# A hybrid GLA and MLA decoder block in float32: one weight sum moved into accumulating transfers, one product order changed, one set of PSUM banks and one gate changed

## Chip, cores and metric

The kernel runs on one core of one Trainium2 chip. The metric is the device time of one execution in microseconds. An execution's time is a little longer than the span of its profile, from the first to the last instruction of the program.

## What is computed

One layer of an autoregressive decoder, with 512 tokens, a width of 1024, in float32 throughout. After a layer norm, two branches run on the same rows: gated linear attention (GLA, 4 heads) and multi-head latent attention (MLA, 8 heads with a nope part of 128 and a rotary part of 64). Each is projected back, the two are merged by sigmoid gates, and one output projection follows; then comes a squared-ReLU MLP. Cut to what matters:

```python
h = layer_norm(x, ln_in_g, ln_in_b)
q_g, k_g, v_g, r_g, a_lr, q_lat, kv_lat, gate_logits = jnp.split(h @ w_in, offsets, axis=-1)
o_gla = gla_chunked(...)                                  # 4 heads, chunks of 64
y_gla = (rms_norm(o_gla) * silu(r_g)) @ w_o_gla
q = (rms_norm(q_lat, q_a_norm_g) @ w_q_b).reshape(bsz, seq, MLA_HEADS, MLA_QK)
q_nope, q_rope = q[..., :128], apply_rope(q[..., 128:], cos, sin)
kv = (rms_norm(kv_lat) @ w_kv_b).reshape(...)             # nope keys and values of 8 heads
y_mla = merge_heads(mla_causal_attention(...)) @ w_o_mla
g_gla, g_mla = jnp.split(jax.nn.sigmoid(gate_logits + b_gate), 2, axis=-1)
h = layer_norm(ALPHA * h + (g_gla * y_gla + g_mla * y_mla) @ w_out)
h = layer_norm(ALPHA * h + jnp.square(jax.nn.relu(h @ w_ff1)) @ w_ff2)
```

## The kernel before, in words

**Split products.** Every float32 operand of a large product is split into a high part, rounded to the matmul's format, and a low part, the rest; a product is three matmuls (high by high, high by low, low by high). `split` and `pump` do this for activations and weights: ScalarE copies the high part, VectorE subtracts it. A row named `whi<-wraw` or `whi<-wq` in the profile is the first half of a weight split, `wlo<-...` the second. There are two `whi` and two `wlo` buffers and three raw ones, so the split of an element of the weight stream can begin when TensorE has finished the element two before it.

**The stream.** All weights pass through one list, `stream`, in the order in which `plan`, `plan_unit`, `plan_qr` and `plan_pair` append to it; the products must be called in the same order. `fetch` issues plain loads on the SP queue ahead of use, and `pump` splits one or two elements ahead. An element may carry `gates`: instructions of ScalarE or VectorE behind which its split is queued. An element may have a `post`, called once its split is issued.

**Seven products in place of eight.** The large square projections, among them GLA's output (`yg`, weights `w_o_gla`), are computed with a Winograd-like scheme: a 2 by 2 block product from seven products, with weight blocks 11, 22, 21 and the sums t1, t2, t3, t4. The sums are formed in the raw tiles (`wq`): t1 and t3 by loading one block and adding another to it with an accumulating transfer (issued by GpSimd, line 1308), t2 by a VectorE addition behind the split of 22 (`u_sum`). For `yg`, t4 is t2 plus block 21; before the change VectorE adds it behind the split of block 21. For the second gate unit (`g1`) t4 is made by `u_acc`, an accumulating transfer of block 21 from HBM onto the tile of t2 (line 412).

**MLA.** For each pair of heads, `mla_pair` makes nope queries, nope keys and values. `mla_qr(g)` makes the rotary queries of four heads: two accumulators are turned by cosine and sine tables on VectorE (rows `rt<-mm,tab`), split, and sent to their places by GpSimd transfers (`QS<-q`). The heads (`mla_head`) are generators that are stepped between products: scores (L1121 to L1132), softmax on VectorE and ScalarE, transposes of the probabilities (L1154, tile `Ps` or `P02`, evicted as `PT`), and outputs (L1175 to L1177).

**PSUM.** There are two pools of four banks: `mm`, for the accumulators of the projections (`MM()`), and `px` (`PX()`), for transposes, scores, attention outputs and some accumulators. The nope keys of the first pair stand in `px`, those of the other three in `mm`.

**Start.** The first layer norm's rows are normalised on ScalarE and VectorE, transposed on TensorE, scaled, and split into `h` by `ln_transpose`, one block of 128 features at a time for 256 tokens. `ln_in1` does this for the second half of the tokens, between the products for the latents.

**What sets the order.** Python's order of calls gives each instruction its priority. When the program is built, the framework orders each engine's instructions by that priority and by its own simulated timeline, gives out buffers and banks, and adds the semaphores. On the chip every engine works through its list in that fixed order. The kernel ties single instructions down with `issue_after`. The order around GLA's last products is, in the stream and in the calls:

```python
    t0, mv = mla_pair(0)
    mv()
    y_gla("21")
    mla_qr(1)
    y_gla("t4")
    t1, mv = mla_pair(1)
```

Of the kernel before, what the change touches and what calls it, by code (L numbers as in the profile page):

```python
# [52 lines left out]
def tile_hybrid_block(ctx: ExitStack, tc: tile.TileContext, I, out, dbg=None):  # L53
# [12 lines left out]
    def nm(s):  # L66
        uid[0] += 1
        return f"{s}_{uid[0]}"
# [18 lines left out]
    def MM(n="mm"):  # L87
        return pm.tile([P, T], F32, tag="mm", name=nm(n))

    def PX(shape=(P, T), dt=F32, n="px"):  # L90
        return px.tile(list(shape), dt, tag="px", name=nm(n))

    def f(ap):
        return ap.bitcast(F32)
# [46 lines left out]
    xt = []  # L141
# [14 lines left out]
    g_in = ca[:, P:P + NK]  # L156
    b_in = ca[:, P + NK:P + 2 * NK]
# [11 lines left out]
    stream = []  # L169
    st = {"dma": 0, "spl": 0, "gates": ()}  # L170
# [75 lines left out]
    def weights(pl, k):  # L246
        i, j = pl["at"][k]
        pump(i)
        hi, lo = stream[i]["w"]
        return hi[:, j, :], lo[:, j, :]  # L250
# [4 lines left out]
    def spawn(g):  # L255
        active.append(g)
        return g
# [22 lines left out]
    def gemm_fm(pl, xs, n, evac, width=None, toks=slice(0, T), accs=None, guard=None, held=False):  # L280
        na = n // P
        accs = accs or [MM() for _ in range(na)]
        for k in range(pl["nk"]):
            hi, lo = weights(pl, k)
            xh, xl = part(xs[k], 0, toks), part(xs[k], 1, toks)
            first, last = k == 0, k == pl["nk"] - 1
            for a in range(na):
                c = slice(a * P, (a + 1) * P)
                o = accs[a][:, toks]
                with ExitStack() as gates:  # L290
                    if last and held:
                        gates.enter_context(tc.issue_after(st["tp"].ins))
                    mm(o, hi[:, c], xh, start=first, stop=False)  # L293
                mm(o, hi[:, c], xl, start=False, stop=False)  # L294
                mm(o, lo[:, c], xh, start=False, stop=last)  # L295
            if not last:
                tick(width)
        if guard:
            guard()
        if evac is not None:  # L300
            for a in range(na):
                evac(a, accs[a])
                if a == na // 2 - 1:
                    pump(pl["idx"][-1] + 1)
        tick(width)
        return accs
# [45 lines left out]
    PL = {}  # L352
# [16 lines left out]
    for op, _ in RW:  # L369
        for hf in range(2):  # L370
            PL["r"].append(len(stream))
            e = {"nk": 2, "n": T, "res": False, "ahead": 2, "home": "wwwwrwrwrwwwrw"[2 * RW.index((op, _)) + hf]}
# [7 lines left out]
    def plan_qr(g):  # L380
        PL["qr", g] = plan("w_q_b", NOPE, 4 * ROPE, heads=(HQ, 4 * g, 4), parts=2)
# [21 lines left out]
    def u_sum(key, a, to, g, x, new=None):  # L403
        src = WQ[key, (a, g)]
        t = WQ[key, (to, g)] = src if new is None else new
        with tc.issue_after(st["lo"].ins):
            vtt(t, src, x, op=ALU.add)


    def u_acc(key, a, to, g, op):  # L410
        t = WQ[key, (to, g)] = WQ[key, (a, g)]
        nc.gpsimd.dma_start(t, u_src(key, int(op[0]) - 1, int(op[1]) - 1, g), accum_op=ALU.add)

    def plan_unit(*seq):
        for key, op in seq:
            for g in range(UNITS[key][2]):
                PL[key, op, g] = len(stream)
                e = {"nk": 4, "n": 256, "res": False}
                if key in ("g1","yg"):
                    e["cut"] = 2  # L420
                if (key, op, g) == ("yg", "t3", 1):
                    e["home"] = "b"
                if op[0] != "t" and (op, key) not in HELD:
                    e["dmas"] = [(slice(0, 4), u_src(key, int(op[0]) - 1, int(op[1]) - 1, g), None)]
                else:
                    e["src"] = lambda q=(key, (op, g)): WQ[q]
                    if key == "g0" and op in ("t1", "t2"):
                        e["ahead"], e["home"] = 2, "wr"[g]
                if op == ("t1" if key == "g0" else "22"):
                    e["post"] = lambda raw, q=(key, "t1", "t2", g): u_sum(*q, WQ[q[0], ("22", q[3])] if q[0] == "g0" else raw)  # L430
                    if key == "f1":
                        e["post2"] = lambda raw, q=(key, "12", "t3", g): u_sum(*q, raw)
                elif op == "21" and key == "yg":
                    e["post"] = lambda raw, g=g: u_sum("yg", "t2", "t4", g, raw)
                elif op == "t2" and key == "g1":
                    e["post"] = lambda raw, g=g: u_acc("g1", "t2", "t4", g, "21")
                elif op == "t2" and key != "yg":
                    e["post2" if key == "f1" else "post"] = lambda raw, q=(key, "t2", "t4", g): u_sum(*q, WQ[q[0], ("21", q[3])])
                stream.append(e)

# [10 lines left out]

    plan_pair(0)
    plan_unit(("yg", "21"))
    plan_qr(1)
    plan_unit(("yg", "t4"))
    plan_pair(1)
    plan_pair(2)
    plan_pair(3)
# [63 lines left out]
    def ln_transpose(rows, g, b, outs, hf, alt=False, n="h0"):  # L522
        tk = slice(hf * 256, (hf + 1) * 256)
        for k in range(NK):
            if len(outs) <= k:
                outs.append(A([P, 2, T], F32R, n) if n == "h0" else (B([P, T], F32R, n), B([P, T], F32R, n)))
            p = MM() if alt and k in (4, 5) else PX()
            for i in range(2):
                tp = nc.tensor.transpose(p[:, i * P:(i + 1) * P], rows[2 * hf + i][:, k * P:(k + 1) * P],
                                         identJ if hf and n == "h0" else ident)  # L530
            if k == 1:
                st["tp"] = tp
            tmp = B([P, 256], F32, "lnt")
            hi, lo = part(outs[k], 0, tk), part(outs[k], 1, tk)
            ha = act(hi, p[:, :256], AF.Identity, scale=g[:, k:k + 1], bias=b[:, k:k + 1])
            if (alt or n == "h1") and k % 2:
                act(tmp, p[:, :256], AF.Identity, scale=g[:, k:k + 1], bias=b[:, k:k + 1])
            else:
                vts(tmp, p[:, :256], g[:, k:k + 1], b[:, k:k + 1], op0=ALU.mult, op1=ALU.add)
            hd = vtt(lo, tmp, f(hi), op=ALU.subtract)  # L540
            if n == "h1":
                st["ln"] = (ha, hd)
            elif hf and k == 5:
                st["h0"] = (ha, hd)
            yield hd

    mvin = consts.tile([P, NT, 2], F32, name="mvin")
    hT = []
# [125 lines left out]
    qlT, ckT, qld, ckd, GL, KKs = [], [], [], [], [], []  # L674
# [413 lines left out]
    def mla_pair(pr):  # L1088
        vt = [None] * NT
        qn = [None] * 2  # L1090
        kn = [None] * 2

        def ev_v(a, j, ps):
            t = B([P, 2, 256], F32R, "mv")
            split(ps[:, :256], t[:, 0, :], t[:, 1, :])
            vt[a] = t

        def ev_n(dst, sc):
            def e(a, ps):
                dst[a] = A([P, 2, T], F32R, "qn")  # L1100
                split(ps, dst[a][:, 0, :], dst[a][:, 1, :], scale=sc)
            return e
        gemm_fm(PL["qn", pr], qlT, 256, ev_n(qn, scale))
        gemm_fm(PL["kn", pr], ckT, 256, ev_n(kn, None), accs=None if pr else [PX(), PX()])
        return ([spawn(mla_head(2 * pr + a, a, qn[a], kn[a], vt)) for a in range(2)],
                lambda guard=None: gemm_tm([PL["mv", pr]], ckT, 256, ev_v, guard=guard))

# [76 lines left out]
    def ln_in1():  # L1184
        for i in range(4):
            yield

        def splits():
            stream[5]["gates"] = (st["var"],)
            pump(4)  # L1190
            chain.update(dve=st["lo"])

        for tt in (2, 3):
            chain.update(dve=st["lo"] if tt == 2 else st["nmr"])
            ln_rows(xt[tt], xt[tt], mvin[:, tt, :], on_act=((0, 1), (0,))[tt - 2], between=splits if tt == 2 else None)
            chain.clear()
            if tt == 3:
                stream[7]["gates"] = (st["var"],)
            yield
            if tt == 2:  # L1200
                yield
        stream[PL["q"]["idx"][0]]["gates"] = (st["norm"],)
        yield from ln_transpose(xt, g_in, b_in, hT, 1, alt=False)

    hsd = []

# [261 lines left out]
    hT = hops = None  # L1468
# [32 lines left out]
    y_gla = unit("yg", yops, ev_y, after_y)  # L1501
# [2 lines left out]
    t0, mv = mla_pair(0)  # L1504
    mv()
    y_gla("21")
    mla_qr(1)
    y_gla("t4")
    ogT = yops = y_gla = None
    t1, mv = mla_pair(1)  # L1510
    mv(lambda: finish(*t0))
    t2, mv = mla_pair(2)
# [56 lines left out]
    accs = gemm_fm(PL["f1", 0, 0], h1T, T, None, toks=slice(0, 256), held=True)  # L1569
# [289 lines left out]
```

## Time and profile before

| what | us |
| --- | --- |
| median of 3 runs (lowest, highest) | 864.10 (864.09, 864.13) |
| the profiled execution's own time | 864.03 |
| its span | 862.2 |
| TensorE matmuls busy | 852.3 (99%) |
| TensorE weight loads busy | 752.8 (87%) |
| VectorE busy | 658.1 (76%) |
| ScalarE busy | 494.0 (57%) |
| GpSimd busy | 136.0 (16%) |
| granted TensorE clock, mean | 0.998 |

Times in the profile count from the first instruction. Matmuls are pipelined and their ends are modelled, so their rows overlap: the step from one start to the next tells more than a row's length. PE is TensorE, PEld its weight loads, DVE VectorE, ACT ScalarE, POOL GpSimd, SP the queue of plain loads. A row of the timeline has start, length, engine, line, operation, output and inputs, shape, count, and in brackets the idle time before it and what ended that. Most VectorE and ScalarE instructions go through one helper and bear its line, L111, so they are told apart by their tiles. The later parts of the program, from the output projection (about 480 us) on, are not touched.

### The profile page before, as it was taken

The numbers are of one execution on the slowest core, as the hardware profiler recorded it, in microseconds if no ns is written. First come the engines' busy times: TensorE is split into PE (matmuls) and PEld (weight loads), VectorE is DVE, ScalarE is ACT, GpSimd is POOL, SyncE is SP. The second block draws the span as 40 slices with busy tenths as digits, with TensorE's granted clock in tenths as the row PEclk, the third lists the DMA queues.
The fourth block names the chain that finished last, engine by engine and source line by source line (L and its number), as shares of the span: only waits on it lengthen the run. The fifth ranks groups of instructions, "written<-read, shape, count | busy, mean of one in ns | idle before, by whom it ended". The sixth has DMA issues, their size and how long they took to land.

```text
span 862.2 us, 13265 instructions
## 1 busy us (share of the span) xinstructions
PE 852.3 (99%) x4887; PEld 752.8 (87%) x4887; DVE 658.1 (76%) x1169; ACT 494.0 (57%) x891; POOL 136.0 (16%) x179
## 2 busy tenths in 40 slices
PE   8999999999999999999999999999999999999996
PEld 7988888889999999988888889888888888889985
DVE  7767889977578968997856879985567546898865
ACT  7456977655576754565645325475466446766810
POOL 1530001010211103030000021005301520141000
PEclk9999999999999999999999999999999999999999
DMA  9995946696649917143146355009922990599312
GB/s 316 233 214 156 341 156 161 211 263 219 148 134 249 211 43 183 44 105 98 42 177 217 115 165 189 1 1 266 256 63 57 299 222 9 107 249 229 112 61 74
DMA packets 101232, 137.94 MB, mean 160 GB/s; under 512 B 13202, under 2 KB 66117, under 8 KB 101169
## 3 DMA queue, kind: packets, MB, share of 16 engines
q1 hardware_dynamic: 76512, 91.35, 33.8%
q0 software_dynamic: 22784, 41.10, 22.9%
q10 hardware_dynamic: 1872, 4.66, 1.5%
q8 instruction: 38, 0.62, 0.3%
q14 instruction: 26, 0.20, 0.1%
HBM read 113.49 MB, written 8.91 MB: 142 GB/s over the span
## 4 chain that ended last, share of the span: by engine, by line
PE 97%; ACT 1%; DVE 1%; DMA 0%; issue 0%; POOLq 0%; POOL 0%; DVEq 0%
PE mm L293 10%; PE mm L295 10%; PE mm L294 10%; PE mm L1335 6%; PE mm L1333 6%; PE mm L1334 6%; PE mm L333 5%; PE mm L331 5%; PE mm L332 5%; PE px L1668 3%; PE px L1667 3%; PE px L1669 3%; PE mm L1668 2%; PE mm L1667 2%; PE mm L1669 2%; PE mm L887 1%
## 5 line engine op out<-in xcount | busy, mean ns | idle before, releaser
L111 DVE TENSOR_TENSOR wlo<-wraw,whi 128x1024 fp32r<-128x1024 f32 (+2 forms) x108 | 96.8, 911 | 63.3 <-ACT whi L111 63.2
L111 ACT ACTIVATE whi<-wraw 128x1024 fp32r<-128x1024 f32 (+2 forms) x108 | 85.1, 806 | 78.7 <-PE mm L294 19.3
L294 PE MATMUL mm<-h,whi 128*128 128x512 f32 x224 | 87.2, 389 | 0.0
L293 PE MATMUL mm<-h,whi 128*128 128x512 f32 x224 | 87.1, 390 | 0.0
L295 PE MATMUL mm<-h,wlo 128*128 128x512 f32 x224 | 83.2, 390 | 0.0
L111 DVE TENSOR_TENSOR wlo<-wq,whi 128x1024 fp32r<-128x1024 f32 (+1 forms) x66 | 63.6, 979 | 25.7 <-ACT whi L111 25.5
L111 ACT ACTIVATE whi<-wq 128x1024 fp32r<-128x1024 f32 (+1 forms) x66 | 55.3, 860 | 31.2 <-PE mm L1334 15.3
L1686 POOL DMA_DIRECT2D res<-ev x42 | 38.5, 1045 | 177.5 <-ACT ev L111 147.5
L1333 PE MATMUL mm<-sh,whi 128*128 128x256 f32 x176 | 49.9, 284 | 0.0
L1334 PE MATMUL mm<-sh,whi 128*128 128x256 f32 x176 | 49.7, 283 | 0.0
L293 PEld LDWEIGHTS mm<-h,whi 128*128 128x128 f32 x224 | 42.1, 188 | 8.7
L295 PEld LDWEIGHTS mm<-h,wlo 128*128 128x128 f32 x224 | 42.0, 188 | 8.7
L294 PEld LDWEIGHTS mm<-h,whi 128*128 128x128 f32 x224 | 42.0, 188 | 8.7
L1335 PE MATMUL mm<-sh,wlo 128*128 128x256 f32 x176 | 49.5, 283 | 0.0
L111 ACT ACTIVATE xh<-wraw 128x1024 fp32r<-128x1024 f32 (+1 forms) x24 | 24.2, 1016 | 25.4 <-PE mm L333 15.1
L111 ACT ACTIVATE relu<-mm 128x512 f32<-128x512 f32 x26 | 15.2, 594 | 37.5 <-PE mm L295 37.5
L111 DVE TENSOR_TENSOR xl<-wraw,xh 128x1024 fp32r<-128x1024 f32 (+1 forms) x24 | 27.9, 1170 | 11.2 <-ACT xh L111 11.1
L1334 PEld LDWEIGHTS mm<-sh,whi 128*128 128x128 f32 x176 | 33.8, 192 | 0.0
L1333 PEld LDWEIGHTS mm<-sh,whi 128*128 128x128 f32 x176 | 33.8, 192 | 0.0
L1335 PEld LDWEIGHTS mm<-sh,wlo 128*128 128x128 f32 x176 | 33.6, 192 | 0.0
L1335 PE MATMUL mm<-h,wlo 128*128 128x256 f32 x112 | 32.1, 287 | 0.0
L1333 PE MATMUL mm<-h,whi 128*128 128x256 f32 x112 | 31.8, 284 | 0.0
(495 smaller groups left out, 2785.6 us busy)
## 6 DMA issues: line engine op xcount, KB each, us to landing
wraw<-in_w_ff_dram SPq DMA_DIRECT2D x36, 512.0 KB, 5.4
wraw<-in_w_in_dram SPq DMA_DIRECT2D x30, 512.0 KB, 5.2
wq<-in_w_ff_dram POOLq DMA_DIRECT2D x26, 512.0 KB, 11.2
res<-ev POOLq DMA_DIRECT2D x42, 256.0 KB, 9.1
wq<-in_w_in_dram POOLq DMA_DIRECT2D x20, 512.0 KB, 9.5
wq<-in_w_in_dram SPq DMA_DIRECT2D x18, 512.0 KB, 8.0
hsd<-hs SPq DMA_DIRECT2D x16, 256.0 KB, 4.2
xr<-hsd SPq DMA_DIRECT2D x16, 256.0 KB, 3.8
```

The lines of the kernel that those rows point to most:

```text
L111: ins = op(*a, **k)
L293: mm(o, hi[:, c], xh, start=first, stop=False)
L294: mm(o, hi[:, c], xl, start=False, stop=False)
L295: mm(o, lo[:, c], xh, start=False, stop=last)
L331: mm(o, xh, hi[:, :n], start=opens, stop=False, skip_group_check=share)
L332: mm(o, xh, lo[:, :n], start=False, stop=False, skip_group_check=share)
L333: mm(o, xl, hi[:, :n], start=False, stop=last, skip_group_check=share)
L1333: mm(oa, hi[:, k, c], xh, start=opens and k == 0 and a == 0, stop=False, skip_group_check=True)
L1334: mm(oa, hi[:, k, c], xl, start=False, stop=False, skip_group_check=True)
L1335: mm(oa, lo[:, k, c], xh, start=False, stop=k == 3, skip_group_check=True)
L1667: mm(o, xh[:, c], hi[:, pp], start=opens, stop=False, skip_group_check=True)
L1668: mm(o, xh[:, c], lo[:, pp], start=False, stop=False, skip_group_check=True)
```

## The change

Four edits.

1. GLA's output: the sum t4 = t2 + block 21 is no longer added by VectorE behind the split of 21. `u_acc` sends two accumulating transfers from HBM (one for each column group, 512 KB each) on GpSimd's queue, behind the split of t2. Block 21 is still loaded plainly for its own product.
2. The product t4 comes directly behind the product 21, in the stream and in the calls, and the second rotary queries behind it.
3. The second pair's nope keys accumulate in two `px` banks in place of two `mm` banks, as the first pair's do.
4. In `ln_in1` the split of the first query weights is queued behind the fourth transposed block of the second token half (its high part on ScalarE, its low part on VectorE), and not behind the last normalisation on ScalarE.

```diff
-                elif op == "21" and key == "yg":
-                    e["post"] = lambda raw, g=g: u_sum("yg", "t2", "t4", g, raw)
-                elif op == "t2" and key == "g1":
-                    e["post"] = lambda raw, g=g: u_acc("g1", "t2", "t4", g, "21")
-                elif op == "t2" and key != "yg":
+                elif op == "t2" and key in ("g1", "yg"):
+                    e["post"] = lambda raw, key=key, g=g: u_acc(key, "t2", "t4", g, "21")
+                elif op == "t2":
...
     plan_unit(("yg", "21"))
+    plan_unit(("yg", "t4"))
     plan_qr(1)
-    plan_unit(("yg", "t4"))
...
             hd = vtt(lo, tmp, f(hi), op=ALU.subtract)
+            st["ha"] = ha
...
-        gemm_fm(PL["kn", pr], ckT, 256, ev_n(kn, None), accs=None if pr else [PX(), PX()])
+        gemm_fm(PL["kn", pr], ckT, 256, ev_n(kn, None), accs=None if pr > 1 else [PX(), PX()])
...
-        stream[PL["q"]["idx"][0]]["gates"] = (st["norm"],)
-        yield from ln_transpose(xt, g_in, b_in, hT, 1, alt=False)
+        for k, hd in enumerate(ln_transpose(xt, g_in, b_in, hT, 1, alt=False)):
+            if k == 3:
+                stream[PL["q"]["idx"][0]]["gates"] = (st["ha"], hd)
+            yield
...
     y_gla("21")
+    y_gla("t4")
     mla_qr(1)
-    y_gla("t4")
```

## The prediction

> **What bounds the kernel now.** I read the page first, then the list of waits for the two halves of TensorE, then busy time by stretch, and last the timeline at the few places where TensorE stood. The page says that TensorE carries the time.
>
> ```profile
> span 862.2 us, 13265 instructions
> ...
> PE 852.3 (99%) x4887; PEld 752.8 (87%) x4887; DVE 658.1 (76%) x1169; ACT 494.0 (57%) x891; POOL 136.0 (16%) x179
> ...
> PE 97%; ACT 1%; DVE 1%; DMA 0%; issue 0%; POOLq 0%; POOL 0%; DVEq 0%
> ```
>
> The profiled execution took 864.03 us, its span 862.2 plus 1.83 around it; the runs have a median of 864.10 (864.09 to 864.13), 0.07 above. I make the sum against 864.03. The change removes no matmul, so it can only win time in which TensorE stands. The waits of the weight loads, which show a stall earlier than the modelled ends of matmuls do, name nearly all of it after the start (one more, at 28 us, has its own rows below):
>
> ```profile
> PEld mm L293 <- ACT PT L111: 0.8, 1, 0.8
> ...
> PEld mm L295 <- DVE wlo L111: 0.4, 1, 0.4
> ...
> PEld px L1175 <- DVE PT L111: 0.4, 1, 0.4
> PEld px L1176 <- DVE PT L111: 0.4, 1, 0.4
> ```
>
> ```profile
> 360.00:370.00 10.00, 9.64 (x58) 8.25 (x56) 9.22 (x21) 5.43 (x11) 0.50 (x1) 1.00 0.19 50
> 370.00:380.00 10.00, 9.75 (x61) 8.93 (x62) 9.01 (x22) 5.86 (x16) 5.17 (x11) 1.00 0.43 110
> 380.00:430.00 50.00, 49.96 (x302) 44.45 (x302) 42.02 (x130) 32.59 (x85) 2.17 (x5) 1.00 0.24 71
> ...
> 850.00:860.00 10.00, 5.43 (x40) 4.99 (x39) 6.93 (x15) 0.00 (x0) 1.19 (x1) 0.97 0.21 76
> ```
>
> The columns are length, then busy time of TensorE, its loads, VectorE, ScalarE and GpSimd, granted clock, DMA share, GB/s. Between 360 and 430 us TensorE lacks 0.65 us in all, nearly all of it in one gap at 370. So the whole prize is about one microsecond of 864: 0.12%. A measurement of this kernel can tell about 0.2%, or 1.73 us, from no change.
>
> **The change, part by part.**
>
> **Second nope keys in PX banks.** At 370 TensorE waits before the first product of the second pair's nope keys:
>
> ```profile
> 362.65 0.60 PE L1154 MATMUL px<-ca,Pm 128*128 128x128 f32 x4
> 363.00 0.47 PE L293 MATMUL mm<-latT,whi 128*128 128x512 f32 x1
> ...
> 366.29 0.39 PE L295 MATMUL mm<-latT,wlo 128*128 128x512 f32 x1
> 366.51 0.39 PE L1175 MATMUL px<-PT,mv 128*128 128x512 f32 x1
> ...
> 369.04 0.60 PE L1154 MATMUL px<-ca,Pm 128*128 128x128 f32 x4
> 370.25 0.47 PE L293 MATMUL mm<-latT,whi 128*128 128x512 f32 x1 [0.61 <-ACT PT L111]
> ```
>
> ```profile
> 363.83 1.28 DVE L111 TENSOR_TENSOR rt<-mm,tab 128x512 f32<-128x512 f32 x2
> ...
> 369.41 1.28 DVE L111 TENSOR_TENSOR rt<-mm,tab 128x512 f32<-128x512 f32 x2
> ...
> 373.01 1.28 DVE L111 SCALAR_TENSOR_TENSOR qn<-mm,qn 128x512 fp32r<-128x512 f32 x2
> ...
> 375.13 0.68 DVE L111 TENSOR_TENSOR qn<-mm,qn 128x512 fp32r<-128x512 f32 x1
> ```
>
> Four transposes and the step to the next product take 0.35 us at 362.65 (363.00 - 362.65) and 1.21 us at 369.04: the wait costs 0.86 us. The profile names ScalarE's PT, but I blame the bank. Of the four mm banks the nope queries just made hold two, and VectorE empties these only from 373.01. The other two hold the second rotary queries, whose last two reads are the pair at 369.41, done at about 370.05 and 370.69. The keys start between the two. In PX banks they depend on neither: -0.86 us. Bounds: nothing (the wait moves) to -0.86.
>
> **Output's last product ahead of the second rotary queries.** The same matmuls, in another order. The product t4 needs its two weight splits earlier:
>
> ```profile
> 343.82 0.42 ACT L111 ACTIVATE whi<-wraw 128x256 fp32r<-128x256 f32 x1 [2.71 <-PE mm L1334]
> 347.38 0.63 ACT L111 ACTIVATE whi<-wraw 128x512 fp32r<-128x512 f32 x1 [3.15 <-PE mm L1334]
> ...
> 350.44 1.14 ACT L111 ACTIVATE whi<-wq 128x512 fp32r<-128x512 f32 x2
> ...
> 353.11 1.14 ACT L111 ACTIVATE whi<-wq 128x512 fp32r<-128x512 f32 x2
> ```
>
> ```profile
> 344.00:348.00 4.00, 4.00 (x31) 3.79 (x30) 2.19 (x5) 0.85 (x3) 0.00 (x0) 1.00 0.37 99
> ```
>
> The rows at 350.44 and 353.11 are these splits; they take the slots of the rows at 343.82 and 347.38, each of which stood idle (2.71 and 3.15 us) until TensorE gave a split buffer back. From 344 to 348 ScalarE works 0.85 of 4.00 us and VectorE 2.19, so 1.14 and twice 0.68 more fit: no cost. The rotary weights' second split now waits for t4's second half. The first rotary queries show its price without cover, the 0.4 us of "L295 <- DVE wlo" above; before, scores filled that hole, and attention work of the first pair is still there to fill it. Bounds 0 to 0.4, I take 0.1. Behind it the rotary multiplications on VectorE come after the next nope queries' split instead of after t4's. They lose the slot from 363.83 if that split comes late, and gain what is saved next; I leave their end near 370.7. Next in line behind them are the QS transfers on GpSimd, read only by the third pair's scores.
>
> **Last sum by accumulating transfers.** Removed are two VectorE additions of 1.22 us; added are two transfers of 512 KB on GpSimd's queue, behind the splits of t2:
>
> ```profile
> L111 DVE TENSOR_TENSOR wq<-wq,wraw 128x1024 f32<-128x1024 f32 x2 | 2.4, 1220 | 0.0
> ```
>
> ```profile
> 313.87 1.29 DVE L111 TENSOR_TENSOR wlo<-wq,whi 128x512 fp32r<-128x512 f32 x2 [1.59 <-ACT whi L111]
> ```
>
> ```profile
> L412 POOL DMA_DIRECT2D wq<-in_w_in_dram x2: 1283/1284/1286, 279.5 to 281.4; - x2
> ```
>
> ```profile
> DMA to landing us min/median/max: 6.0/11.3/15.1
> ```
>
> ```profile
> 327.51 0.57 POOL L1084 DMA_DIRECT2D QS<-q  x1 [35.06 <-ACT q L111]
> ```
>
> ```profile
> 312.00:322.00 10.00, 10.00 (x73) 8.95 (x72) 5.84 (x12) 5.14 (x10) 0.00 (x0) 1.00 0.16 46
> 322.00:330.00 8.00, 8.00 (x61) 7.58 (x60) 7.02 (x12) 3.81 (x8) 0.57 (x1) 1.00 0.61 189
> ```
>
> The second half of t2 is split by 315.2 (313.87 + 1.29); its transfer issues for 1.28 us (the gate's own accumulation, L412) and lands at worst 15.1 us later (the longest of the other accumulations), at 331.6. Its first reader cannot start before the buffer of 343.8 comes free: 12 us to spare. GpSimd had been idle for 35.06 us before 327.51, so nothing queues behind it. The 1.05 MB meet a DMA share of 0.16, then 0.61; a weight load pushed back there has its split some microseconds later, so I take 0, with 0 to +0.4 for bounds. Without that cover it would cost up to 15.1 us. The 2.44 us that VectorE saves lie at 339 to 343, where TensorE waits for nothing: 0 directly, but they let VectorE reach 350 with less queued.
>
> **First query split behind the fourth transposed block.** ScalarE splits a weight before the first block of normalised tokens:
>
> ```profile
> 26.45 1.04 ACT L111 ACTIVATE whi<-wraw 128x1024 fp32r<-128x1024 f32 x1
> ...
> 27.95 1.92 ACT L111 ACTIVATE h<-px,ca 128x256 fp32r<-128x256 f32 x4
> ```
>
> ```profile
> 27.98 0.32 PE L332 MATMUL mm<-xl,h 128*128 128x360 f32 x1
> 28.15 0.33 PE L333 MATMUL mm<-xh,h 128*128 128x360 f32 x1
> 28.56 0.43 PE L331 MATMUL mm<-xh,h 128*128 128x360 f32 x1
> ...
> 45.96 0.39 PE L293 MATMUL mm<-h,whi 128*128 128x512 f32 x1
> ```
>
> A step is 0.17 us (27.98 to 28.15), and 0.41 where TensorE waits for h: 0.24 lost. Moved behind four blocks the 1.04 us no longer stand ahead of that first block: -0.24. The later blocks keep their place, for the split still precedes them. Its reader is the first query product at 45.96, some 14 us later. The raw buffer comes free some 4 us later too; what is loaded into it is read only behind that product. Bounds 0 to -0.24.
>
> **Sum:** 864.03 - 0.86 + 0.1 - 0.24 = 863.03; with the 0.07 to the median, 863.1 us.
>
> **The rivals.**
>
> (a) **The wait moves.** The attention uses the four PX banks for scores, transposes and outputs. Or the value product, which still needs two mm banks, now waits for the rotary reads. For: VectorE is busy 9.22 and 9.01 of 10 at 360 to 380, and its order is set when the program is built. Against: the keys' twelve products fill 2.6 us (12 x 0.22, the step from 366.29 to 366.51), and with them TensorE has work past 370.69. If 0.86 is paid again elsewhere the time is 863.9; up to 1.9 us more it is still no measurable change, 863.7 to 865.8.
>
> (b) **PX banks run short: slower.** Place: 366 to 376. VectorE empties the second key bank at 375.8 (375.13 + 0.68). If the keys keep two of the four PX banks from 366.5 until then, the second head's ten transposes get at most the rest, while TensorE has, by the column at 0.22 us for 512, 2.6 us of keys, 1.65 of the first head's outputs (three each of 512, 384, 256 and 128 columns) and 2.6 of values (24 of 256): 6.9 in all, to 373.4. A wait of 2.4 us until 375.8, and then 0.68 for a first split of the transposes freed so late, cost 3.1: 866.2. It decides once the loss exceeds 2.8 us (the 1.0 won and the 1.73). Against: ScalarE and VectorE may empty these banks sooner, because less is queued.
>
> (c) **That wait grows long enough to slow the clock.** The rows hold the granted clock at 1.00 through the 0.86 us wait, and show 0.97 only at the end, where TensorE is idle for 4.57 of 10 us. A wait of 4 us followed by 2 us more of work at a lower rate would give 869.
> The Trainium skill, "TensorE: Matmul & The Clock Gate", section "Why this matters for your kernels", says to leave no idle gap above about 3 us between bursts, as an idle window halves the clock. By that rule the 1 us in my sum costs no clock, and only a wait such as (b)'s at its worst would; the trace agrees as far as its 0.86 us goes, and no row here shows a gap of 3 us inside the work.
>
> (d) **More is won.** The two 0.4 us waits for PT, in the later attention, go too because VectorE is 2.4 us ahead: 862.3 or less.
>
> **How the numbers follow.** My forecast, 862.4 to 863.6, has a chance of 0.55; (a) 0.27; (b) 0.10; (c) 0.02; (d) 0.06. The likeliest is 863.1. The range runs from 862.3, the start of (d), to 865.3, most of (a), so that (b), (c) and the tails, under 2 in 10, lie outside. Faster by over 0.2% (below 862.37) is (d): 0.06; slower (above 865.83) is (b) and (c): 0.12; within 0.2% the rest: 0.82.
>
> **What would show it.** The wait of L293 on PT should be gone from the list and 360 to 380 should show TensorE at 19.9 of 20 or more; the key evictions should read px; no wait of 1 us or more should stand at scores, transposes or value products up to 390. The two additions of 1.22 us at 339 to 343 should be gone, two more accumulations should issue near 312 to 316, and the splits of t4 should begin near 344, not wait for a DMA. At 28 us the step of 0.41 should be 0.17. A wait for a px bank, or rotary reads that end well after 371 with a product behind them, would make me wrong.

## The result, and the profile after

The changed kernel takes 865.58 us (median of 16 runs, 865.22 to 866.88), the kernel before 864.12 on the same chip: a ratio of 1.0016, 95% interval 1.0009 to 1.0023. So it is slower, by 0.16%, which is less than the 0.2% named above as the bound of a measurable change; the time is 2.5 us above the forecast of 863.1 and 0.3 above the upper end of the range, 865.3. The profiled execution took 865.70 us; its span is 863.62, with 2.08 around it. (Before, the span is 862.24 unrounded, with 1.79 around it.)

The page of the changed kernel: the same matmuls, a longer span, and 27 packets on the instruction queue q14, where the page before has 26.

```profile
span 863.6 us, 13266 instructions
...
PE 853.2 (99%) x4887; PEld 753.0 (87%) x4887; DVE 656.4 (76%) x1167; ACT 494.9 (57%) x891; POOL 139.0 (16%) x181
...
q14 instruction: 27, 0.21, 0.1%
```

Its waits of the weight loads. Lines of the kernel shift a little from run to run: the transposes of L1154 and the outputs of L1175 to L1177 are L1153 and L1174 to L1176 here, and have numbers up to four higher in the runs below. The wait of L293 on PT is gone, as forecast. In its place the outputs of the second head (L1174, and one of the two waits of L1175) wait.

```profile
PEld px L1174 <- ACT PT L111: 1.1, 1, 1.1
PEld px L1175 <- DVE PT L111: 0.7, 2, 0.4
```

The same stretches as before the change: from 360 to 380 TensorE is busy for 19.03 of 20 us, and had been for 19.39.

```profile
360.00:370.00 10.00, 10.00 (x56) 8.35 (x54) 8.00 (x21) 5.54 (x14) 0.00 (x0) 1.00 0.30 81
370.00:380.00 10.00, 9.03 (x56) 7.99 (x56) 9.37 (x17) 6.44 (x14) 1.69 (x4) 1.00 0.20 53
380.00:430.00 50.00, 49.96 (x304) 44.42 (x304) 42.66 (x133) 32.15 (x87) 6.17 (x13) 1.00 0.27 80
```

And the timeline where it stands (`omT` is a head's finished output, evicted from PSUM):

```profile
369.42 0.60 PE L1153 MATMUL px<-ca,Pm 128*128 128x128 f32 x4
369.49 0.60 ACT L111 ACTIVATE omT<-px 128x512 fp32r<-128x512 f32 x1 [1.94 <-PE px L1176]
369.98 1.08 ACT L111 ACTIVATE PT<-px 128x512 fp32r<-128x512 f32 x2
370.12 0.69 DVE L111 TENSOR_TENSOR omT<-px,omT 128x512 fp32r<-128x512 f32 x1 [0.65 <-ACT omT L111]
370.73 1.28 DVE L111 TENSOR_TENSOR PT<-px,PT 128x512 fp32r<-128x512 f32 x2
...
370.96 0.47 PE L1174 MATMUL px<-PT,mv 128*128 128x512 f32 x1 [0.94 <-DVE omT L111]
...
371.46 0.50 PE L1175 MATMUL px<-PT,mv 128*128 128x512 f32 x1
...
372.22 0.39 PE L293 MATMUL px<-latT,whi 128*128 128x512 f32 x1
...
374.65 0.69 DVE L111 TENSOR_TENSOR rt<-mm,tab 128x512 f32<-128x512 f32 x1
```

Behind the four transposes comes the second head's first output, not a key. Four transposes and the step to it take 1.54 us where 0.35 would do (1.19 lost), and the next step 0.50 where 0.22 would do (0.28): 1.47 in place of the 0.86 before. Two things end the first wait. ScalarE's half of PT, which the product reads, is there at 370.57; the profile names VectorE's read of the first head's output (omT, done at 370.81), which gives a px bank back, as the one that came last. The keys, in px banks, come at 372.22, when the wait is over.

I cut each profile at four places: the first transposes of x, the last matmul's start, VectorE's last instruction's end, the end of the span. Between the two profiles the difference of 1.67 (865.70 - 864.03) is then 0.32 ahead of the first transposes (8.13 against 7.81 us, the first load of x), 0.68 in TensorE's work, nothing from the last matmul to VectorE's end (4.14 us in both), 0.37 between VectorE's end and the span's, and 0.29 around the span.

### The profile page after: what moved, and what is told of

Its sections match the earlier page's. It is cut to its first block, busy times and chain, and to the rows that moved or that the text cites. A ratio compares the mean times of both kernels' runs of the same rounds, so it can differ in the third digit from the quotient of the medians.

```text
span 863.6 us, 13266 instructions
## 1 busy us (share of the span) xinstructions
PE 853.2 (99%) x4887; PEld 753.0 (87%) x4887; DVE 656.4 (76%) x1167; ACT 494.9 (57%) x891; POOL 139.0 (16%) x181
## 4 chain that ended last, share of the span: by engine, by line
PE 97%; DVE 1%; ACT 1%; DMA 0%; issue 0%; POOLq 0%; POOL 0%; DVEq 0%
PE mm L293 10%; PE mm L295 10%; PE mm L294 10%; PE mm L1336 6%; PE mm L1334 6%; PE mm L1335 6%; PE mm L333 5%; PE mm L331 5%; PE mm L332 5%; PE px L1668 3%; PE px L1670 3%; PE px L1669 3%; PE mm L1668 2%; PE mm L1670 2%; PE mm L1669 2%; PE mm L888 1%
## 5 line engine op out<-in xcount | busy, mean ns | idle before, releaser
L293 PE MATMUL mm<-h,whi 128*128 128x512 f32 x224 | 87.3, 390 | 0.0
L293 PEld LDWEIGHTS mm<-h,whi 128*128 128x128 f32 x224 | 42.0, 188 | 8.7
```

## The experiments

Two theories for TensorE's part. **The order theory (O):** when the program is built, the change of order puts the second head's outputs straight behind its transposes, and the keys that used to cover the transposes' eviction behind them. **The bank theory**, that of the prediction: the keys stand because mm banks are still being read. For the end of the execution: **theory F**, the number of instructions on the SP queue, against **theory V**, the number on VectorE. All are told by this table. "Work" is from the first transposes of x to the last matmul's start, "end" from VectorE's last instruction to the end of the span, both in the profiled execution. "Count" is VectorE's instructions in the trace, waits for semaphores included. "Packet" is when the last but one 8 KB packet of the instruction queue q14 moved, counted from the end of VectorE's last instruction; the ones ahead of it moved some 85 us before that end, and the very last one moves behind the end of the span in every kernel (at +3.95 to +5.33). The first two rows are the 16 runs above; each other kernel was timed in 11 runs, and its ratio is to the kernel before in the same batch (863.86 to 864.20).

| kernel | median us | ratio (95%) | work | end | count | packet |
| --- | --- | --- | --- | --- | --- | --- |
| before (profile above) | 864.12 | | 847.34 | 2.95 | 1472 | +3.86 |
| after (profile above) | 865.58 | 1.0016 (1.0009 to 1.0023) | 848.02 | 3.32 | 1474 | +1.81 |
| px_alone | 865.55 | 1.0016 (1.0007 to 1.0024) | 848.46 | 3.17 | 1473 | +3.50 |
| swap_alone | 865.36 | 1.0012 (1.0003 to 1.0021) | 848.44 | 2.96 | 1475 | -0.76 |
| acc_alone | 864.30 | 1.0002 (0.9993 to 1.0011) | 847.38 | 3.01 | 1471 | +4.09 |
| gate_alone | 864.39 | 1.0003 (0.9994 to 1.0012) | 848.07 | 2.95 | 1471 | +4.04 |
| after_again | 865.34 | 1.0012 (1.0003 to 1.0021) | 847.98 | 3.36 | 1474 | +1.81 |
| no_px | 865.66 | 1.0018 (1.0009 to 1.0027) | 849.27 | 3.33 | 1474 | +1.81 |
| b_rfirst | 864.10 | 0.9999 (0.9990 to 1.0009) | 848.00 | 2.94 | 1475 | -0.75 |
| noPx_rfirst | 864.95 | 1.0011 (1.0002 to 1.0020) | 848.11 | 3.01 | 1472 | +3.96 |
| after_sp2 | 865.38 | 1.0016 (1.0007 to 1.0025) | 849.89 | 3.70 | 1474 | +1.82 |
| b_rheld | 863.68 | 0.9995 (0.9986 to 1.0004) | 847.06 | 2.95 | 1475 | -0.75 |
| after_dve1 | 864.75 | 1.0009 (1.0000 to 1.0018) | 847.58 | 3.01 | 1475 | -0.76 |
| before_dve2 | 864.21 | 1.0003 (0.9994 to 1.0012) | 847.42 | 3.32 | 1474 | +1.81 |

Single profiles carry a stall that the others of the same order lack: 0.5 to 1.8 us in the work of gate_alone, no_px, b_rfirst and after_sp2. The medians tell of kernels, the waits of a profile tell where.

**px_alone**: edit 3 on the kernel before.

```diff
-        gemm_fm(PL["kn", pr], ckT, 256, ev_n(kn, None), accs=None if pr else [PX(), PX()])
+        gemm_fm(PL["kn", pr], ckT, 256, ev_n(kn, None), accs=None if pr > 1 else [PX(), PX()])
```

> The kernel before with only edit 3 (second nope keys in two px banks). By the prediction's own step the 0.86 us wait at 370 goes: 863.2. Theory O (the order that the build gives TensorE decides): here the 24 value products stand directly behind the second head's last transposes, where the keys stood; they need two mm banks, which the second rotary queries' reads still hold, so the wait stays at 370 and only changes its name: 864.0 to 864.3. Theory B (the px banks run short, rival b): a wait of over 1 us for a px bank at the second head's outputs or at the keys, 864.8 or more.

Measured: 865.55, 1.35 above before (864.20 in that batch). Its timeline:

```profile
369.30 0.60 PE L1154 MATMUL px<-ca,Pm 128*128 128x128 f32 x4
370.50 0.35 PE L331 MATMUL mm<-whi,latT 128*128 128x256 f32 x1 [0.60 <-ACT PT L111]
...
402.95 0.27 PE L1154 MATMUL px<-ca,Pm 128*128 128x128 f32 x1
403.47 0.50 PE L1175 MATMUL px<-PT,mv 128*128 128x512 f32 x1 [0.25 <-ACT PT L111]
404.32 0.50 PE L1176 MATMUL px<-PT,mv 128*128 128x512 f32 x1 [0.35 <-DVE PT L111]
```

With the keys in px banks the build puts the 24 value products behind the transposes. They need the mm banks that the keys had needed, and stand just as long: 1.20 for a step of 0.35, 0.85 lost. The wait has changed its place in the list, from the keys (L293) to the value products (L331). Later the second pair's outputs stand behind their transposes without cover: 0.46 at 403.47 and 0.63 at 404.32 (steps of 0.52 and 0.85 where 0.06 and 0.22 would do). That sum of 1.09 is nearly the whole 1.12 by which the work is longer. So the forecast's largest gain, by itself, is a loss. Theory O had the first wait right, but no theory held the second one, and the time lies 1.25 us above its 864.0 to 864.3. Theory B's 864.8 or more fits the time, but not the place: the outputs at 403 and 404 are put down to PT, which they read, and neither wait is over 1 us.

**swap_alone**: edit 2 alone (the two lines of the order, in the stream and in the calls).

```diff
     plan_unit(("yg", "21"))
+    plan_unit(("yg", "t4"))
     plan_qr(1)
-    plan_unit(("yg", "t4"))
...
     y_gla("21")
+    y_gla("t4")
     mla_qr(1)
-    y_gla("t4")
```

> The kernel before with only edit 2 (t4 directly behind 21, second rotary queries behind t4; the sum still added by VectorE). By the prediction's step: 864.2, since only the 0.1 of an uncovered split is added. Theory O: TensorE's order now has the second head's outputs directly behind its transposes, before any key product, so it stands for the evictions of the first head's output and of the first transposes: about 1.5 us at 369 to 372 in place of 0.86, 864.8 to 865.6, as in the changed kernel, although the keys are in mm banks. Theory B: 864.2, as no px bank was given away.

Measured: 865.36.

```profile
369.06 0.60 PE L1154 MATMUL px<-ca,Pm 128*128 128x128 f32 x4
370.60 0.47 PE L1175 MATMUL px<-PT,mv 128*128 128x512 f32 x1 [0.94 <-DVE omT L111]
371.10 0.50 PE L1176 MATMUL px<-PT,mv 128*128 128x512 f32 x1
...
372.19 0.28 PE L1175 MATMUL px<-PT,mv 128*128 128x256 f32 x1
372.90 0.50 PE L293 MATMUL mm<-latT,whi 128*128 128x512 f32 x1 [0.43 <-DVE qn L111]
```

The wait of the changed kernel is here without edit 3: 1.19 at 370.60 and 0.28 at 371.10. Then the keys, still in mm banks, wait 0.59 for the nope queries to be read (0.71 for a step of 0.12). The sum, 2.06, is 1.2 more than the 0.86 before; the work is 1.10 longer. So the order makes the loss, as theory O says, and the 1.19 at the first output is the same whether the keys hold px banks or not.

**acc_alone**: edit 1 alone.

```diff
-                elif op == "21" and key == "yg":
-                    e["post"] = lambda raw, g=g: u_sum("yg", "t2", "t4", g, raw)
-                elif op == "t2" and key == "g1":
-                    e["post"] = lambda raw, g=g: u_acc("g1", "t2", "t4", g, "21")
-                elif op == "t2" and key != "yg":
+                elif op == "t2" and key in ("g1", "yg"):
+                    e["post"] = lambda raw, key=key, g=g: u_acc(key, "t2", "t4", g, "21")
+                elif op == "t2":
```

> The kernel before with only edit 1 (t4 by two accumulating transfers). TensorE's order around 370 is that of the kernel before. Prediction and theory O: 864.0 to 864.2. If the added transfers were what cost time (other loads late, or a longer start or end of the execution), 864.5 or more, with a weight load waiting for a split at 320 to 345 or a first load of x longer than 3.6 us.

Measured: 864.30, no difference that shows, and a work of 847.38 against 847.34.

**gate_alone**: edit 4 alone.

```diff
             hd = vtt(lo, tmp, f(hi), op=ALU.subtract)
+            st["ha"] = ha
...
-        stream[PL["q"]["idx"][0]]["gates"] = (st["norm"],)
-        yield from ln_transpose(xt, g_in, b_in, hT, 1, alt=False)
+        for k, hd in enumerate(ln_transpose(xt, g_in, b_in, hT, 1, alt=False)):
+            if k == 3:
+                stream[PL["q"]["idx"][0]]["gates"] = (st["ha"], hd)
+            yield
```

> The kernel before with only edit 4 (first query split behind the fourth block). By the prediction's step: 863.9, with the step of 0.41 at 28 us down to 0.17. By what the changed kernel's trace shows (ScalarE's eviction of lat stands between the split and h and starts when TensorE is done with lat, not when the split is): the step stays 0.41, and the time is 864.0 to 864.2.

Measured: 864.39, no difference that shows, and the step is 0.41 still (28.37 to 28.78 us). ScalarE in the changed kernel, which shows the same, and TensorE behind it:

```profile
27.92 0.47 ACT L111 ACTIVATE lat<-mm 128x360 f32<-128x360 f32 x1 [1.05 <-PE mm L333]
28.29 1.47 ACT L111 ACTIVATE h<-px,ca 128x256 fp32r<-128x256 f32 x3
```

```profile
28.49 0.33 PE L333 MATMUL mm<-xh,h 128*128 128x360 f32 x1
28.90 0.43 PE L331 MATMUL mm<-xh,h 128*128 128x360 f32 x1
```

The split has gone, ScalarE is idle for 1.05 us in its place, and the step is still 0.41. Ahead of h stands another instruction, the eviction of a latent, and that begins when TensorE has made it. Before, this row stood between the split and h too (kernel before, ScalarE), and my rows had left it out:

```profile
27.58 0.47 ACT L111 ACTIVATE lat<-mm 128x360 f32<-128x360 f32 x1
```

**after_again** (the changed kernel once more) and **no_px** (the changed kernel with `None if pr` again in edit 3).

> The changed kernel as it is, a second time, beside the runs below: 865.4 to 865.7. Its profile is a second look at what lies outside TensorE's work: the first profile had the first product of x at 8.13 us (7.81 before), 3.32 us from the last VectorE instruction to the end of the span (2.95 before), and 2.1 us around the span (1.83 before). If these are chance, they fall back here; if they belong to the kernel, they stay. The waits of 1.15 and 0.28 us at the second head's outputs must come back in either case.

> The changed kernel without edit 3 (second nope keys in mm banks again; the other three edits stay). Theory O: the outputs' wait of 1.15 and 0.28 us stays, since it comes from the order, and the keys behind them wait another 0.6 us for the nope queries' banks, as in the run with edit 2 alone: 865.2 to 866.2, not faster than the changed kernel. Theory B (the px banks given to the keys cost the time): 864.0 to 864.5.

Measured: 865.34 and 865.66. The waits at the outputs, the end of 3.36 and the packet at +1.81 came back in after_again; the later start did so in part (7.94 us). The waits of no_px:

```profile
PEld px L1174 <- ACT PT L111: 1.1, 1, 1.1
...
PEld mm L293 <- DVE qn L111: 0.7, 1, 0.7
```

So, given the new order, edit 3 saves the second wait (0.59 as in swap_alone). The medians, 0.32 apart, have intervals that overlap, so that gain rests on the trace.

**b_rfirst**: the kernel before, with the four rotary multiplications, which read the mm banks, issued ahead of the additions and the split.

```diff
-            for i, (x, y, op) in enumerate(((ps[0], ps[1], ALU.subtract), (ps[1], ps[0], ALU.add))):
-                t1 = B([P, T], F32, "rt1")
-                t2 = B([P, T], F32, "rt2")
-                with tc.issue_after(st["lo"].ins):
+            ops = ((ps[0], ps[1], ALU.subtract), (ps[1], ps[0], ALU.add))
+            ts = [[B([P, T], F32, n) for n in ("rt1", "rt2")] for _ in ops]
+            for (t1, t2), (x, y, op) in zip(ts, ops):
+                with ExitStack() as tie:
+                    if True:
+                        tie.enter_context(tc.issue_after(st["lo"].ins))
                     vtt(t1, x, cos, op=ALU.mult)
                     vtt(t2, y, sin, op=ALU.mult)
-                    vtt(t1, t1, t2, op=op)
+            for i, (x, y, op) in enumerate(ops):
+                t1, t2 = ts[i]
+                vtt(t1, t1, t2, op=op)
```

> The kernel before, with the four multiplications of the second rotary queries by the tables (the only reads of their two mm banks) issued together, ahead of the first addition. The prediction's bank theory: the banks come free near 366.5 in place of 370.7, the wait of 0.86 us before the keys at 370 is gone, and the time is 863.2 to 863.6; some 0.3 of it may come back at the first head's outputs, whose PT halves VectorE makes 1.2 us later. The rival (ScalarE's eviction of PT ends that wait, as the list of waits names it): a wait of 0.8 stays before the keys, 864.0 to 864.4.

Measured: 864.10, the same as before (864.02 there). Its timeline on VectorE, then on TensorE:

```profile
364.50 2.48 DVE L111 TENSOR_TENSOR rt<-mm,tab 128x512 f32<-128x512 f32 x4
```

```profile
372.49 0.60 PE L1158 MATMUL px<-ca,Pm 128*128 128x128 f32 x4
373.46 0.49 PE L1179 MATMUL px<-PT,mv 128*128 128x512 f32 x1 [0.37 <-ACT PT L111]
374.19 0.50 PE L1180 MATMUL px<-PT,mv 128*128 128x512 f32 x1 [0.23 <-DVE PT L111]
```

The banks are read by 366.98, and no key waits any more: so the bank theory named rightly what held the keys, though the time is that of its rival (864.0 to 864.4). One doubt stays in this run, for here the keys run ahead of the transposes, where no PT is in their way. The trace of the kernel before speaks for the bank there too: the first of the two rotary reads ends at 370.10 and the key's weight load starts 0.12 later, just as the changed kernel's first output starts 0.12 behind omT (370.81, 370.93); ScalarE's PT ends at 370.20, only 0.02 ahead of that load, where a product that does wait for PT starts 0.05 behind it (here 373.41, 373.46). But now the keys run early, and the transposes at 372.49 have none behind them: 0.62 and 0.51 are lost at the outputs. Twelve keys that can run at any time are cover, and cover spent early is missed later.

**noPx_rfirst**: no_px with the same rotary edit.

> The changed kernel without edit 3, and with the four multiplications of the second rotary queries issued together. TensorE's order has one product of the second head's outputs behind the transposes, then all twelve key products, then the other outputs. Theory O: that one product still waits 1.15 us for the px bank of the first head's output (VectorE's eviction near 370.1 to 370.8), the 0.28 and the 0.6 behind it go: 864.5 to 865.1. If the order were not the cause, the time would be that of the kernel before or below: 863.3 to 864.2.

Measured: 864.95, 0.71 below no_px. VectorE, then TensorE:

```profile
368.38 1.28 DVE L111 TENSOR_TENSOR rt<-mm,tab 128x512 f32<-128x512 f32 x2
...
370.52 1.28 DVE L111 TENSOR_TENSOR rt<-mm,tab 128x512 f32<-128x512 f32 x2
```

```profile
369.21 0.60 PE L1157 MATMUL px<-ca,Pm 128*128 128x128 f32 x4
370.75 0.47 PE L1178 MATMUL px<-PT,mv 128*128 128x512 f32 x1 [0.94 <-DVE omT L111]
371.26 0.50 PE L293 MATMUL mm<-latT,whi 128*128 128x512 f32 x1
```

The build did not keep the four together: an eviction came between the pairs. The first key still waits for a rotary read (0.51 for a step of 0.22, 0.28 lost, in place of 0.59), and the first output still stands for 1.19 behind the transposes. Of the 0.71 that it is faster than no_px, some 0.3 is the end (3.01 against 3.33), at a VectorE count of 1472 in place of 1474. Banks set free sooner don't mend the order.

**b_rheld**: b_rfirst, and of the second pair's twelve keys the six of the second weight block held behind the second head's last transposes (`held` now names the instruction behind which the last block is tied).

```diff
-                        gates.enter_context(tc.issue_after(st["tp"].ins))
+                        gates.enter_context(tc.issue_after(st[held].ins))
...
-        gemm_fm(PL["kn", pr], ckT, 256, ev_n(kn, None), accs=None if pr else [PX(), PX()])
+        gemm_fm(PL["kn", pr], ckT, 256, ev_n(kn, None), accs=None if pr else [PX(), PX()], held="ph" if pr == 1 else False)
...
-                nc.tensor.transpose(p[:, cc * P:(cc + 1) * P], Ps[i][:, j * P:(j + 1) * P],
-                                    identJ if i > 1 else ident)
+                st["ph"] = nc.tensor.transpose(p[:, cc * P:(cc + 1) * P], Ps[i][:, j * P:(j + 1) * P],
+                                               identJ if i > 1 else ident)
...
-    accs = gemm_fm(PL["f1", 0, 0], h1T, T, None, toks=slice(0, 256), held=True)
+    accs = gemm_fm(PL["f1", 0, 0], h1T, T, None, toks=slice(0, 256), held="tp")
```

> The kernel before, with the four multiplications of the second rotary queries together, and the six key products of the second weight block tied behind the second head's last transposes. Theory O and the bank theory together: the keys no longer wait for a bank (0.8), and 1.4 us of them stand behind the transposes again, so that the outputs' waits (0.58 and 0.50 in the run with the multiplications alone) shrink to some 0.2 in all: 863.2 to 863.7, faster than the kernel before. If products behind the transposes do not cover the evictions, those waits stay: 864.0 to 864.2.

Measured: 863.68. The timeline on TensorE:

```profile
370.92 0.66 PE L1158 MATMUL px<-ca,Pm 128*128 128x128 f32 x4 [0.15 <-DVE Pm L111]
371.33 0.47 PE L293 MATMUL mm<-latT,whi 128*128 128x512 f32 x1
...
372.80 0.40 PE L1179 MATMUL px<-PT,mv 128*128 128x512 f32 x1
373.32 0.50 PE L1180 MATMUL px<-PT,mv 128*128 128x512 f32 x1
```

With six keys between the transposes and the outputs, the first output waits for nothing, and the second loses 0.30 (0.52 for a step of 0.22). The keys start 0.41 behind the transposes, so PT does not hold them. The other six keys run ahead of the transposes and leave them to wait: 0.32 is lost there for VectorE's Pm, the probabilities to be transposed (a step of 0.55 for 0.23). In all 0.62 stands in place of 0.86, and the work is 0.28 shorter than before the change, the shortest of all. The ratio of 0.9995 has an interval (0.9986 to 1.0004) that takes in 1, so the expected gain on the kernel before isn't shown by the times; the interval lies below that of the changed kernel's 16 runs (from 1.0009), and just meets that of after_again (from 1.0003). This is theory O run the other way: cover put where the wait is takes most of the wait away.

**after_sp2**: the changed kernel with two transfers of 64 bytes more on the SP queue, behind the first finished rows of the output.

```diff
+        if tt == 0:
+            for i in range(2):
+                nc.sync.dma_start(DR([1, 16], "pad"), r[i:i + 1, :16])
```

> The changed kernel with two tiny extra transfers (64 bytes each, to a scratch in HBM) on the SP queue behind the first finished output rows; every engine's order is otherwise the same. Theory F (a fetch of instructions falls into the end): in both profiles of the changed kernel, and in that of the one without edit 3, an 8 KB packet of an instruction queue lies 1.81 us behind VectorE's last instruction, SP has 459 instructions, and the end is 3.3 us long; in the others SP has 460 to 462, no such packet lies there, and the end is 2.95 to 3.2. Two more SP instructions then bring the end back to about 3.0 and what lies around the span from 2.05 to 1.8: 864.8 to 865.0, with the waits of 1.15 and 0.28 us unchanged. If the longer end belongs to the edits themselves: 865.3 to 865.6, as before.

Measured: 865.38, with the packet at +1.82 and an end of 3.70. Theory F had the packet move and the end shorten to 3.0, and neither did: for the end, F fell. Its other figure came true: what lies around the span fell from 2.01 (mean of the changed kernel's 16 runs, 1.88 to 2.13) to 1.77 (11 runs, 1.73 to 1.82). The longer end took that gain away again.

**after_dve1** and **before_dve2**: one VectorE memset of 128x1 more at the start of the changed kernel, two of them at the start of the kernel before.

```diff
     nc.vector.memset(f(still), 0.0)
+    pad = consts.tile([P, 1], F32, name="pad")
+    nc.vector.memset(pad, 0.0)
```

> The changed kernel with one more VectorE instruction (a 128x1 memset of an unused tile, at the start, where VectorE waits for x); every order is otherwise the same. Theory V (the place of a fetch of VectorE's instructions decides the end): in the twelve profiles so far VectorE has 1471 to 1473 instructions where the last 8 KB instruction packet comes 3.5 us or more behind its last instruction, 1475 where it comes 0.75 us ahead of it, and 1474, in the changed kernel and its near copies alone, where it falls at 1.8 us, into the end, which is then 3.3 us or more. With 1475 the packet should come at -0.75, the end take 2.95, and the time be 864.8 to 865.0. Rival: the longer end has another cause in the edits: 865.3 to 865.6.

> The kernel before with two more VectorE instructions (128x1 memsets of unused tiles, at the start); every order is otherwise the same. Theory V: 1474 instructions, the instruction packet at 1.8 us behind the last one, an end of 3.3 us in place of 2.95 and some 0.25 more around the span: 864.5 to 864.8, slower than the kernel before though no step of its work changed. Rival: 863.9 to 864.2.

Measured: 864.75 (ratio 1.0009 where the changed kernel has 1.0012 to 1.0016) and 864.21 (863.86 for before in the same batch). By the medians, one instruction more makes the slower kernel faster, and two make the faster one a little slower; the intervals overlap, so the packets and ends decide. These came as theory V had them (-0.76 and 3.01; +1.81 and 3.32). Its time for before_dve2, 864.5 to 864.8, did not: the 0.25 more around the span, which it took over from the changed kernel, stayed away (1.79). The 2 us behind VectorE's end, first of the changed kernel, then of after_dve1, by DMA:

```profile
DMA  0849989898996969899999998999997310003000
...
q14 instruction: 1, 0.01, 1.0%
...
out_dram<-res SPq DMA_DIRECT2D x1, 128.0 KB, 2.4
```

```profile
DMA  0649979999899698999999999999720000000000
...
q1 hardware_dynamic: 288, 0.39, 52.8%
q10 hardware_dynamic: 144, 0.13, 18.9%
...
out_dram<-res SPq DMA_DIRECT2D x1, 128.0 KB, 1.9
```

Forty slices of 0.05 us: the changed kernel has an instruction packet in slice 37 (the 3, at +1.8 us), and its last output lands 2.4 us after its issue; after_dve1 has none there, and 1.9. Before_dve2 shows what the changed kernel does (the kernel before has 2.1 at most):

```profile
DMA to landing us min/median/max: 2.0/2.1/2.4
```

So theory V holds both ways for the packet and the end, and the end costs 0.37 (3.32 - 2.95). That is about what before_dve2 loses by its median (0.35), though its ratio alone does not tell it from no change. The trace also tells where in the end it lies: the last output lands 2.38 us after its issue in place of 2.01, and from there to the end of the span it is 0.91 in both kernels. Of the 0.6 to 0.8 by which after_dve1 is faster than the changed kernel's medians, 0.3 is the end and 0.4 a shorter work in that profile, with the same waits at the outputs.

## Why the prediction was wrong

- **"In PX banks they depend on neither: -0.86 us."** This step failed. The cause named for the old wait, the bank, was right (b_rfirst), but the keys were not only the waiter, they were also the cover of the eviction behind the transposes. The build reorders TensorE's products around them: with edit 3 alone the value products took the wait over (0.85) and the outputs lost 1.09 more; with edit 2 the outputs took it over (1.47). Bounds of "nothing (the wait moves) to -0.86" were wrong at the upper end, for a wait that moves can grow: the two edits together make +0.61 of it. Between -0.86 and +0.61 lie 1.47 of the 2.48 us by which the forecast missed.
- **"The same matmuls, in another order", 0.1.** The hidden cost of the order was not the weight split but the place of the second head's outputs. The splits of t4 waited for TensorE alone, as forecast (ScalarE in the changed kernel):

```profile
344.79 1.16 ACT L111 ACTIVATE whi<-wq 128x512 fp32r<-128x512 f32 x2 [3.39 <-PE mm L1335]
```

  The four transposes start 0.38 later than before (369.42 against 369.04). Of that 0.32 is the start, so 0.06 was lost up to there, near the 0.1 that I took.
- **"I leave their end near 370.7."** The second rotary reads began at 374.65, behind the omT and PT evictions. By itself this cost nothing here, since the keys no longer needed those banks.
- **Accumulating transfers, 0.** Right. They issued at 312.85 and 315.73 and landed 8.0 us later at worst, and edit 1 alone leaves the work as it was:

```profile
312.85 1.28 POOL L412 DMA_DIRECT2D wq<-in_w_o_gla_dram  x1 [20.27 <-DVE wlo L111]
315.73 1.28 POOL L412 DMA_DIRECT2D wq<-in_w_o_gla_dram  x1 [1.60 <-DVE wlo L111]
```

- **Gate, -0.24.** Wrong: 0. The split was ahead of h, but a latent's eviction stood between them and waited for TensorE, so taking the split away left ScalarE idle. That is 0.24 more of the miss.
- **The rivals.** (a) came true in kind: the wait moved. It did not stay at 0.86. That the time falls into its wide 863.7 to 865.8 is in part luck, since 0.6 of it comes from the end and the time around the span, which (a) did not hold. (b) had the place right (366 to 376) and the px banks, but the outputs waited, for the bank of omT and for PT, not the transposes, and for 1.2 us, not 2.4; and the keys in px banks are not what made it, since swap_alone has the same wait without them. (c) did not come: the clock column stays at 1.00 in both stretches. (d) did not come.
- **What no case held:** the end of the program, and the time around the span. The change left VectorE two instructions more in the trace (two additions fewer, four waits for semaphores more), and 0.37 of the 1.67 us between the two profiles is what the end took longer. The time around the span grew too, from 1.77 to 1.79 (means of the kernel before in its later batches) to 2.01 (mean of the changed kernel's runs). Each of two edits does that alone: acc_alone has 1.93 and gate_alone 1.97, while their spans have the same median as before (862.4 in that batch), which is why both medians lie 0.1 to 0.2 above what was expected; px_alone and swap_alone have 1.78 and 1.79. It goes with the number of instructions on the SP queue: all kernels with 462 have 1.77 to 1.79, those with 459 have 1.94 to 2.01, and those with 460 or 461 have 1.82 to 1.97; after_sp2 moved the changed kernel from the second group to the first.

What stays open: why the SP queue's count changes the time around the span. The start, 0.32 later in one profile and 0.13 in that of after_again, differs from run to run (7.50 to 8.13 us over all kernels) and is not shown to be the change's.

## What to carry to other kernels

A product that waits may at the same time be the one that covers the next eviction. Before freeing it, ask what the build will put in its place, and look for the cover of each eviction (here 1.0 to 1.5 us passed from the first of the transposes to the first product that reads what they made, where nothing stood between). Where the order is made at build time, run each edit alone: here the one that promised most lost as much by itself as the four together, and holding six products back was worth more in the traces than giving them other banks. Of differences of some tenths of a microsecond, look at the end of the program and at the time around the span before explaining them.

## What the runs showed of the hardware

The end of this kernel's execution depends on how many instructions VectorE has. With 1471 or 1472 the last but one q14 packet moved some 4 us after VectorE's last instruction, with 1473 at +3.50, with 1474 at +1.81 and with 1475 before it (-0.76). Only at 1474 does it fall while the last output is on its way, and there the end took 3.3 to 3.7 us in place of 2.9 to 3.2, in five profiles out of five. In all five the last output landed 2.4 us after its issue, in the others after 1.9 to 2.0. Why a packet of 8 KB should hold the output up for that long is not shown.

The Trainium skill, "Runtime: NRT & Kernel Launch", section "Instruction fetch mechanics", has each engine fetch its instructions in 16 KiB blocks at a cost that is mostly hidden. Here the large packets of q14 are 8 KB each, and the one at the end was not hidden: it went with 0.37 us.
